# Attention of a two-layer hybrid block: one score product per head, exponentials turned by TensorE, values as the stationary operand

## The chip, the cores and the metric

The kernel runs on one core of a Trainium2 chip. The metric is the device time of one execution in microseconds (us). A core has TensorE (PE in the rows; its weight loads are PEld), VectorE (DVE), ScalarE (ACT), GpSimd (POOL) and SyncE (SP). TensorE takes both operands from SBUF and writes its products to PSUM, of which there are eight banks of 128 x 512 fp32 values. Two number formats matter here: `F32R`, with which a product is one TensorE instruction, and `F32`, with which a product shows as two instructions in the trace.

## The reference, cut to what matters

The model has two layers over 256 context tokens and 256 latent tokens of width 1024. A layer is a SwiGLU block, a mixer and a SwiGLU block. The mixer has three groups: attention (512 features, 8 query heads of 64, 2 key/value heads), a gated linear recurrence (LRU, 256 features) and a short convolution (256 features). In layer 0 both streams have queries; in layer 1 only the latent one has.

```python
def attend(q, k, v):
    s = jnp.einsum('bqkgd,bskd->bkgqs', q, k, preferred_element_type=jnp.float32) * ATTN_SCALE
    p = jax.nn.softmax(s, axis=-1).astype(v.dtype)
    return jnp.einsum('bkgqs,bskd->bqkgd', p, v)

def merge_groups(parts, g, w_out):
    return jnp.concatenate([_rms(t) for t in parts], axis=-1) * g @ w_out
...
    k_all = jnp.concatenate([kc, kx], axis=1)     # 256 context keys, then 256 latent keys
    attn_x = blocked_attention(qx, k_all, v_all)  # latent queries: 512 keys
...
    attn_c = attend(qc, kc, vc)                   # context queries: 256 keys, layer 0 only
```

## The kernel before

Activations lie with features on the partitions and tokens along the free dimension: columns 0 to 255 are the context (`CS`, s = 0), 256 to 511 the latent tokens (`XS`, s = 1). An fp32 product of weights and activations is made of three `F32R` products of high and low parts (`mm3`, L326 to L330), so nearly all TensorE work of the kernel stands in lines 328 to 330. Every weight block of 128 x 1024 is loaded by SP, then split by ACT (high part, L120) and DVE (low part, L121), two blocks ahead of its use.

A mixer is a list of steps in an order written out by hand (`ORDER`, L27 to L35); every engine's instructions follow that list, apart from small interchanges that the framework makes when it lays the engines' queues out ahead of time. The steps around the change are: `sc` the convolution's three projections per feature tile, `qc` the turning of queries, `ga` and `ge` the gates of the LRU, `lr` and `ls` its roots and scans, `me` the norms of LRU (1) and convolution (0), `op` the share of these two groups in the output projection (needs both `me`). `kT` holds the keys as [high; high] and [low; low], `qT` the queries as [high; low], both with head features on the partitions, so that two `F32R` products make a score.

The attention steps of one stream and head, before:

- `mx` (`maxima`, L788): scores with queries on the partitions and keys along the free dimension, for four heads; DVE takes the negative maximum over the keys (L802) and nothing else of them is kept.
- `mr` (`max_rows`, L806): the maxima are turned into rows by TensorE (L814) and copied by ACT (L817).
- `sm` (`softmax`, L820): the scores a second time, now with keys on the partitions (L828), plus a third product of 8 rows that adds the head's maximum (L830, `sel` and `mrows`); ACT takes the exponential (L832).
- `va` (`values`, L836): the exponentials are the stationary operand, `vp` (64 values and a column of ones) the moving one, 65 columns wide (L845), both in `F32`. The last head of four divides by the sum (L852, L853).
- `rn` (`row_norm`, L856) and `co` (`columns`, L870): the group's norm with tokens on the partitions, then four turns back to features on the partitions (L876), gains and the split into high and low parts.

After the steps come the attention group's products of the output projection (`out_attn`, L924), first for the context, then for the latent stream.

Of the kernel before, what the change touches and what calls it, by code (L numbers as in the profile page):

```python
# [25 lines left out]
# the order of a mixer's steps after its first products, by layer  # L26
ORDER = ((  # L27
# [8 lines left out]

# columns of the packed per-feature parameters
# [43 lines left out]
def plan():  # L81
    # the first two modules: features 512.. by products ("p"), the others as all modules
# [12 lines left out]
def hybrid_block_kernel(ctx: ExitStack, tc, wpk, xin, pp, cc, cct, qkg, rope, lruw, ident, out):  # L95
# [116 lines left out]
    def lru_consts():  # L212
        # -8 softplus(-lam), halved:  softplus(y) = max(y, 0) + log1p(exp(-|y|))
# [850 lines left out]
```

## Time and profile before

| what | value |
|---|---|
| time, median of 3 runs | 1772.7 us (1772.56 to 1773.01) |
| span of the profiled execution, first to last instruction | 1770.9 us |
| what lies around that span, against the median | 1.8 us |
| PE busy in the span | 1733.4 us (98%) |
| DVE, ACT busy in the span | 1111.8 us (63%), 644.0 us (36%) |
| attention of layer 0, first `mx` to the end of `co` | 484.06 to 624.06 us |
| attention of layer 1, first `mx` to the end of `op` | 1449.39 to 1550.30 us |

All rows come from one profiled execution, and times in them count from the start of its span. A matmul's busy time in the groups of instructions includes its latency, and matmuls overlap; how long one holds TensorE is read from the chain of waits, which gives each piece of time to one instruction. The granted clock of TensorE is given as a share: 1.00 is 2.4 GHz, 0.50 is 1.2 GHz, and a stretch with both shows a number between.

### The profile page before, as it was taken

Reading aid. Unit: us, or ns where it says so; the run is one execution under the profiler, and the core shown is the slowest. Engines: PE = TensorE matmul, PEld = TensorE weight load, DVE = VectorE, ACT = ScalarE, POOL = GpSimd, SP = SyncE. Lnnn points to the kernel's source line nnn. Section 1 sums busy time; section 2 is a strip of 40 time slices with the busy share of each in tenths; the row PEclk is TensorE's granted clock in tenths of the full one; section 3 lists DMA queues with packets and bytes.
Section 4 is the critical chain, followed back from the end, with each engine's and each line's share of the span. In section 5 each row is a group of like instructions: output and inputs, shape, how many; then the busy total and the mean of one; then the engine's idle time right before and its main releaser. Section 6 shows DMA issues by size and latency. Waiting matters only on the chain.

```text
span 1770.9 us, 22767 instructions
## 1 busy us (share of the span) xinstructions
PE 1733.4 (98%) x9098; PEld 1475.1 (83%) x9098; DVE 1111.8 (63%) x1872; ACT 644.0 (36%) x967; POOL 0.2 (0%) x4
## 2 busy tenths in 40 slices
PE   7999999999999999999999999999999989999997
PEld 2888888888877898888888898888888877889997
DVE  5977666776754276685667665754565685265555
ACT  5332122325832253322223343212232474254343
POOL 0000000000000000000000000000000000000000
PEclk9999999999987799999999999999999996699999
DMA  7465544552210024554454434443444221035551
GB/s 284 166 202 191 181 161 170 190 179 96 85 46 1 25 72 147 172 196 162 156 183 170 157 107 143 168 153 133 149 147 166 87 98 55 24 129 200 184 181 46
DMA packets 67938, 246.28 MB, mean 139 GB/s; under 512 B 7668, under 2 KB 8180, under 8 KB 67576
## 3 DMA queue, kind: packets, MB, share of 16 engines
q1 hardware_dynamic: 66816, 243.82, 40.1%
q8 instruction: 71, 1.16, 0.3%
q10 hardware_dynamic: 1016, 1.01, 0.2%
q14 instruction: 35, 0.29, 0.0%
HBM read 243.76 MB, written 1.05 MB: 138 GB/s over the span
## 4 chain that ended last, share of the span: by engine, by line
PE 92%; DVE 4%; ACT 2%; DMA 1%; issue 0%; ACTq 0%; DVEq 0%; SPq 0%
PE ps L328 27%; PE ps L329 27%; PE ps L330 27%; PE ps L845 3%; PE ps L828 2%; PE ps L830 2%; PE ps L799 1%; PE ps L376 1%; DVE junk L253 1%; DVE lo L121 1%; PE ps L749 1%; ACT hh L408 1%; DMA xT<-in_xin_dram 1%; DVE hl L409 1%; DVE ht L407 0%; ACT hi L120 0%
## 5 line engine op out<-in xcount | busy, mean ns | idle before, releaser
L120 ACT ACTIVATE hi<-raw 128x1024 fp32r<-128x1024 f32 x310 | 327.3, 1060 | 799.2 <-PE ps L329 589.0
L328 PE MATMUL ps<-hh,hi 128*128 128x512 f32 (+1 forms) x1664 | 574.9, 352 | 9.2 <-ACT hh L408 9.1
L329 PE MATMUL ps<-hl,hi 128*128 128x512 f32 (+1 forms) x1664 | 582.3, 351 | 1.1 <-DVE hl L409 0.9
L330 PE MATMUL ps<-hh,lo 128*128 128x512 f32 (+1 forms) x1664 | 579.5, 350 | 0.0
L121 DVE TENSOR_TENSOR lo<-raw,hi 128x1024 fp32r<-128x1024 f32 x310 | 378.1, 1222 | 202.3 <-ACT hi L120 201.5
L328 PEld LDWEIGHTS ps<-hh,hi 128*128 128x128 f32 x1664 | 313.0, 191 | 53.4 <-ACT hh L408 12.6
L329 PEld LDWEIGHTS ps<-hl,hi 128*128 128x128 f32 x1664 | 317.0, 191 | 44.1 <-DVE hl L409 3.3
L330 PEld LDWEIGHTS ps<-hh,lo 128*128 128x128 f32 x1664 | 317.2, 191 | 40.2
L253 DVE SCALAR_TENSOR_TENSOR junk<-raw,cb 128x1024 bf16<-128x1024 f32 x272 | 321.1, 1218 | 12.1 <-DMA raw<-in_wpk_dram 12.0
L328 PE MATMUL ps<-gh,hi 128*128 128x512 f32 (+1 forms) x770 | 267.4, 347 | 0.0
L329 PE MATMUL ps<-gl,hi 128*128 128x512 f32 (+1 forms) x770 | 266.9, 347 | 0.0
L330 PE MATMUL ps<-gh,lo 128*128 128x512 f32 (+1 forms) x770 | 266.8, 347 | 0.0
L487 DVE TENSOR_TENSOR gf<-gf,ps 128x512 f32<-128x512 f32 (+1 forms) x88 | 54.5, 619 | 180.1 <-PE ps L330 179.0
L329 PEld LDWEIGHTS ps<-gl,hi 128*128 128x128 f32 x770 | 145.8, 189 | 18.3
L328 PEld LDWEIGHTS ps<-gh,hi 128*128 128x128 f32 x770 | 145.8, 189 | 18.2
L330 PEld LDWEIGHTS ps<-gh,lo 128*128 128x128 f32 x770 | 145.8, 189 | 18.0
L417 DVE SCALAR_TENSOR_TENSOR xT<-ps,modT,xT 128x256 f32<-128x256 f32 x160 | 72.4, 479 | 91.4 <-PE ps L330 90.5
L408 ACT ACTIVATE hh<-ht,modT 128x256 fp32r<-128x256 f32 x88 | 41.9, 504 | 70.4 <-DVE ht L407 69.8
L845 PEld LDWEIGHTS ps<-vp,P 128*128 128x128 f32 x320 | 61.8, 295 | 2.4 <-issue 1.4
L845 PE MATMUL ps<-vp,P 128*128 128x65 f32 x320 | 62.6, 379 | 0.0
L357 ACT ACTIVATE sq<-xT 128x256 f32<-128x256 f32 (+1 forms) x62 | 29.0, 486 | 73.5 <-DVE xT L417 73.2
L121 DVE TENSOR_TENSOR gl<-gf,gh 128x512 fp32r<-128x512 f32 (+1 forms) x88 | 54.4, 618 | 0.7 <-ACT gh L120 0.7
(192 smaller groups left out, 1336.5 us busy)
## 6 DMA issues: line engine op xcount, KB each, us to landing
raw<-in_wpk_dram SPq DMA_DIRECT2D x456, 512.0 KB, 3.3
xT<-in_xin_dram SPq DMA_DIRECT2D x2, 1024.0 KB, 9.6
lw<-in_lruw_dram SPq DMA_DIRECT2D x2, 512.0 KB
cb<-in_cc_dram SPq DMA_DIRECT2D x2, 512.0 KB, 3.6
out_dram<-y SPq DMA_DIRECT2D x2, 256.0 KB, 2.6
out_dram<-y ACTq DMA_DIRECT2D x2, 256.0 KB, 2.6
pps<-in_pp_dram ACTq DMA_DIRECT2D x1, 138.0 KB, 4.6
qkb<-in_qkg_dram ACTq DMA_DIRECT2D x1, 128.0 KB
```

The source lines that it names most:

```text
L120: act(hi, src, AF.Copy)
L121: tt(lo, src, f(hi), OP.subtract)
L253: stt(junk, raw, 1.0, CB[v], op0=OP.mult, op1=OP.mult, accum_out=mod_col(l, m, t, v))
L328: nc.tensor.matmul(ps, wh, xh, start=first, stop=False)
L329: nc.tensor.matmul(ps, wh, xl, start=False, stop=False)
L330: nc.tensor.matmul(ps, wl, xh, start=False, stop=last)
L408: act(hh[:, a:b], t[:, a:b], AF.Identity, bias=mod_col(l, 3 * n, k, v))
L417: stt(xT[:, k, a:b], ps[:, a:b], mod_col(l, m, k, v), xT[:, k, a:b], op0=OP.mult, op1=OP.add)
L487: tt(gf[:, a:b], gf[:, a:b], pu[:, a:b], OP.mult)
L828: nc.tensor.matmul(o, kT[2 * g + z][:, kc:kc + 128], qT[s, hd], start=z == 0, stop=False)
L830: nc.tensor.matmul(o, sel[:, hd % 4, :], mrows[s, g], start=False, stop=True)
L845: nc.tensor.matmul(pv[s][t][:, j * 65:(j + 1) * 65], p[:, t * 128:(t + 1) * 128], vp[:, kt, g], start=kt == 0, stop=kt == len(P) - 1)
```

## The change

Scores are computed once per head (`scores`), with queries on the partitions, as `maxima` did. DVE takes the negative maximum of the bank, and ACT takes the exponential out of the same bank with that maximum as its bias, and sums each row as it goes (`accum_out`). `max_rows`, the second score products, the 8-row products and `sel` are gone. For a pair of heads (`turned`) TensorE turns the exponentials, 128 x 128 at a time, so that keys lie on the partitions, four into a bank; ACT and DVE copy the banks to SBUF by turns. The values are now the stationary operand: `vz` holds the 64 values of a key tile between two blocks of 64 zeros, and a window of 128 columns over it puts a head's output on the lower or the upper 64 partitions. The moving operand is the turned exponentials of two heads, 512 columns wide, in `F32`; two pairs of a key/value head add up in one bank (`values`). The output thus has features on the partitions at once. The inverse row sums are spread over 64 features each, turned (`inverses`) and multiplied in (`merge_attn`), which then takes the group's norm with products of ones, like the other groups, and splits. The order of the steps is written anew from the first score step on.

```diff
 ORDER = ((
...
-    "cv0 cv1 kv0 kv1 ga0 ga1 ga3 ga2 qp0 qp1 kr ge0 ge1 qp2 qp3 qr0 lr sc0 sc1 kc ls0 sc2 qc0 qr1 mx0 sc3 "
-    "sc4 sc5 mr0 sm0 sm2 mx1 va0 qc1 mr1 sm1 sm4 va2 sm3 ls1 sm7 va1 me1 sm6 sm5 va3 va4 mx2 me0 mr2 sm8 "
-    "va5 sm10 sm9 mx3 op0 mr3 va6 sm11 sm12 va8 op1 va9 va7 sm15 op2 va10 op3 op4 sm14 sm13 rn0 va11 va12 "
-    "va14 va13 co0 va15 rn1 op5 op6 op7 co1"),
+    "cv0 cv1 kv0 kv1 ga0 ga1 ga3 ga2 qp0 qp1 kr ge0 ge1 qp2 qp3 qr0 lr sc0 sc1 kc ls0 sc2 qc0 qr1 sm0 sc3 "
+    "sm2 sm1 tr0 sc4 sm3 sm4 va0 sc5 tr1 sm6 qc1 sm5 va1 tr2 ls1 sm7 sm8 va2 tr3 me1 sm10 sm9 va3 nr0 tr4 "
+    "sm11 rn0 sm12 va4 tr5 me0 sm14 sm13 va5 tr6 op0 sm15 va6 tr7 nr1 op1 op2 va7 op3 rn1 op4 op5 op6 op7"),
     (
-    "cv0 kv0 kv1 kr qp0 qp1 qp2 qp3 qr1 ga0 qc1 sc0 cv1 sc1 ge0 sc2 kc ga1 mx0 sc3 ga3 ga2 sc4 sc5 mr0 "
-    "mx1 ge1 sm3 sm0 sm1 sm2 lr mr1 ls0 va0 va1 me0 ls1 sm6 sm5 sm4 va2 va3 sm7 va4 va6 me1 va5 op0 va7 "
-    "op1 rn0 op2 op3 co0 op4 op5 op6 op7"))
+    "cv0 kv0 kv1 kr qp0 qp1 qp2 qp3 qr1 ga0 qc1 sc0 cv1 sc1 ge0 sc2 kc ga1 sm0 sc3 ga3 ga2 sm2 sc4 sm1 tr0 sc5 "
+    "sm3 ge1 sm4 va0 tr1 lr sm6 sm5 va1 tr2 ls0 sm7 me0 va2 tr3 ls1 nr0 me1 op0 va3 op1 rn0 op2 op3 op4 op5 op6 op7"))
...
-    vp = const.tile([128, 4, NKV, 65], F32, name="vp")
-    vec.memset(vp[:, :, :, 64:65], 1.0)
...
+    vz = const.tile([128, 4, NKV, 192], F32, name="vz")
+    nc.gpsimd.memset(vz, 0.0)
...
             nc.tensor.matmul(st[:, a:b], ones[n], x[:, a:b], start=i == 0, stop=i == len(parts) - 1)
+        return rstd_tail(st, cols)
+
+    def rstd_tail(st, cols):
+        a, b = cols
         r0, r1 = T(name="r0"), T(name="r1")
...
-                    act(vp[:, t, :, 0:64], pk[t][:, 128:256].rearrange("p (s d) -> p s d", s=2), AF.Copy)
+                    act(vz[:, t, :, 64:128], pk[t][:, 128:256].rearrange("p (s d) -> p s d", s=2), AF.Copy)
...
-        def maxima(s, hd):
...
-        def max_rows(s, hd):
...
-        def softmax(s, hd):
...
-        def values(s, hd, P):
...
-        def row_norm(s):
...
-        def columns(s):
...
+        def heads(p):
+            g, z = p // 2, p % 2
+            return g, z, (4 * g + z, 4 * g + 2 + z)
...
+        def scores(s, hd):
+            g = hd // 4
...
+            nb = const.tile([128, 2], F32, tag="nb", name="nb", bufs=6)
+            w = 256 if s == 0 else 512
+            n = 512 // w
+            P[s, hd] = []
+            for i in range(0, 2, n):
+                ps = bank()
+                for j in range(n):
+                    q = qT[s, hd][:, (i + j) * 128:(i + j) * 128 + 128]
+                    for z in range(2):
+                        nc.tensor.matmul(ps[:, j * w:(j + 1) * w], q, kT[2 * g + z][:, 0:w], start=z == 0, stop=z == 1)
+                vec.tensor_reduce(nb[:, i:i + n], ps.rearrange("p (i c) -> p i c", i=n), axis=AX.X, op=OP.max, negate=True)
+                p = T(name="P")
+                for j in range(n):
+                    act(p[:, j * w:(j + 1) * w], ps[:, j * w:(j + 1) * w], AF.Exp, bias=nb[:, i + j:i + j + 1],
+                        accum_out=sums[s][:, i + j, hd:hd + 1])
+                    P[s, hd].append(p[:, j * w:(j + 1) * w])
+
+        def turned(s, p):
+            hds = heads(p)[2]
+            PT[s, p] = []
+            for k in range(2 if s == 0 else 4):
+                ps = bank()
+                for j, hd in enumerate(hds):
+                    for i in range(2):
+                        c = j * 256 + i * 128
+                        nc.tensor.transpose(ps[:, c:c + 128], P[s, hd][i][:, k * 128:(k + 1) * 128], idf)
+                t = T(name="PT")
+                if flip[0] % 2:
+                    vec.tensor_copy(t, ps)
+                else:
+                    act(t, ps, AF.Copy)
+                flip[0] += 1
+                PT[s, p].append(t)
+
+        def values(s, p):
+            g, z, _ = heads(p)
+            if z == 0:
+                pv[s, g] = bank()
+            pts = PT.pop((s, p))
+            for k, t in enumerate(pts):
+                nc.tensor.matmul(pv[s, g], vz[:, k, g, 64 - 64 * z:192 - 64 * z], t,
+                                 start=z == 0 and k == 0, stop=z == 1 and k == len(pts) - 1)
+
+        def inverses(s):
+            r = const.tile([128, 2, NH, 1], F32, tag="ri", name="ri", bufs=2)
+            vec.reciprocal(r[:, :, :, 0], sums[s])
...
+            for i, x in enumerate((e, e2)):
+                act(x.rearrange("p (h d) -> p h d", h=NH), r[:, i].to_broadcast([128, NH, 64]), AF.Copy)
+            rec[s] = []
+            for g in range(2):
+                ps = bank()
...
+                        nc.tensor.transpose(ps[:, c:c + 128], x[:, k * 128:(k + 1) * 128], idf)
+                t = T(name="rec")
+                act(t, ps, AF.Copy)
+                rec[s].append(t)
+
+        def merge_attn(s):
+            a, b = parts[s]
+            ot, sq = [], []
+            for g in range(2):
+                o, x = T(name="ot"), T(name="sq")
+                tt(o, pv.pop((s, g)), rec[s][g], OP.mult)
+                act(x, o, AF.Square)
...
+            st = bank()
+            for i, x in enumerate(sq):
+                nc.tensor.matmul(st[:, 0:256], ones[512], x, start=i == 0, stop=i == 3)
...
+                rs = rstd_tail(st, (0, 256))
+            for k, o in enumerate(ot):
+                stt(o, o, grn[:, l, k:k + 1], rs[:, 0:256], op0=OP.mult, op1=OP.mult)
+                split(mg[k][0][:, a:b], mg[k][1][:, a:b], o)
...
-            "mx": lambda i: maxima(*items[4 * i]), "mr": lambda i: max_rows(*items[4 * i]),
-            "sm": start, "va": lambda i: values(*items[i], P.pop(i)), "lr": lambda i: lru_roots(), "ls": lru_scan,
-            "rn": lambda i: row_norm(items[8 * i][0]), "co": lambda i: columns(items[8 * i][0]),
+            "sm": lambda i: scores(*items[i]), "tr": lambda i: turned(*pairs[i]), "va": lambda i: values(*pairs[i]),
+            "nr": lambda i: inverses(pairs[4 * i][0]), "rn": lambda i: merge_attn(pairs[4 * i][0]),
+            "lr": lambda i: lru_roots(), "ls": lru_scan,
```

## Rows read from the trace of the kernel before

**Rows 1.** Profile page: TensorE's granted clock in 40 slices, the chain's shares by engine
```profile
PEclk9999999999987799999999999999999996699999
...
PE 92%; DVE 4%; ACT 2%; DMA 1%; issue 0%; ACTq 0%; DVEq 0%; SPq 0%
```

**Rows 2.** Attention stretches: us; busy PE, PEld, DVE, ACT, POOL (count); clock; DMA share; GB/s
```profile
484.06:624.06 140.00, 137.56 (x618) 109.42 (x619) 61.75 (x135) 44.82 (x85) 0.00 (x0) 0.82 0.09 31
1449.39:1550.30 100.91, 100.86 (x456) 83.37 (x455) 47.71 (x95) 44.12 (x80) 0.00 (x0) 0.68 0.13 42
```

**Rows 3.** Chain of waits, shares by line: 484.06 to 624.06 us, then 1449.39 to 1550.30
```profile
by line: PE ps L845 23.3%; PE ps L828 15.4%; PE ps L830 11.9%; PE ps L328 10.2%; PE ps L329 9.7%; PE ps L330 9.7%; PE ps L799 9.3%; PE ps L376 3.8%; PE ps L876 1.8%; DVE nb L802 1.8%; PE ps L683 1.0%; DVE uc L890 0.9%; DVE ml L121 0.4%; DVE
by line: PE ps L845 25.7%; PE ps L828 20.3%; PE ps L830 14.8%; PE ps L328 7.7%; PE ps L799 7.3%; PE ps L329 6.9%; PE ps L330 6.9%; PE ps L749 4.3%; PE ps L376 3.6%; PE ps L876 0.9%; ACT mh L120 0.4%; PE ps L814 0.4%; DVE uc L890 0.4%; DVE o
```

**Rows 4.** Chain pieces (start us, us, what): softmax products, then value products, two clocks
```profile
510.83 0.43 PE ps L828 x2
511.27 0.31 PE ps L830
...
583.92 1.73 PE ps L845 x16
...
1520.83 7.02 PE ps L845 x32
```

**Rows 5.** Chain pieces: F32R 512 and 256 wide, F32 turns, F32 512 wide
```profile
1422.26 0.23 PE ps L330
...
432.02 0.12 PE ps L329
...
623.18 0.88 PE ps L876 x8
...
436.22 6.87 PE ps L749 x16
```

**Rows 6.** Groups of instructions: busy us, mean ns of one, idle before them
```profile
L832 ACT ACTIVATE P<-ps 128x512 f32<-128x512 f32 x40 | 23.4, 596 | 48.5 <-PE ps L830 48.5
L802 DVE TENSOR_REDUCE nb<-ps 128x1 f32<-128x512 f32 x32 | 20.5, 682 | 9.6 <-PE ps L799 9.6
...
L859 ACT ACTIVATION_READ_ACCUMULATOR sq<-orow 128x1 f32 x6 | 1.1, 188 | 0.0
```

**Rows 7.** Busy time by stretch: early and late part of each attention
```profile
484.00:512.00 28.00, 27.94 (x159) 23.53 (x159) 24.63 (x52) 12.95 (x26) 0.00 (x0) 1.00 0.28 95
512.00:624.00 112.00, 109.56 (x460) 85.83 (x460) 37.12 (x83) 31.87 (x61) 0.00 (x0) 0.77 0.04 15
1449.40:1470.00 20.60, 20.60 (x120) 16.88 (x118) 18.76 (x33) 18.60 (x29) 0.00 (x0) 1.00 0.39 128
1470.00:1550.00 80.00, 79.94 (x336) 66.18 (x336) 28.93 (x63) 25.39 (x51) 0.00 (x0) 0.59 0.06 20
```

**Rows 8.** Order of time, layer 1: the LRU's table load on ACT, its last DVE step
```profile
1467.64 1.28 ACT L572 ACT_TABLE_LOAD   x1
...
1498.71 0.42 DVE L782 SCALAR_TENSOR_TENSOR uc<-uc,ge 128x256 f32<-128x256 f32 x1
```

**Rows 9.** Busy time and clock: F32 gates of layer 0, attention of layer 1
```profile
436.20:443.10 6.90, 6.90 (x18) 3.07 (x17) 2.56 (x3) 6.80 (x12) 0.00 (x0) 1.00 0.79 287
...
1474.30:1539.10 64.80, 64.75 (x226) 52.47 (x226) 15.83 (x36) 16.49 (x37) 0.00 (x0) 0.50 0.03 9
```

**Rows 10.** Chain pieces: turns and value products around the clock's rise
```profile
611.02 0.85 PE ps L876 x4
...
612.19 0.85 PE ps L876 x4
613.05 1.86 PE ps L845 x12
```

**Rows 11.** Order of time, PE in layer 1: an idle gap; chain piece after it
```profile
1434.08 0.81 PE L683 MATMUL ps<-idr,qr 128*128 128x128 f32 x4 [5.12 <-DVE qr L121]
...
1436.29 0.21 PE ps L328
```

More of the change, by code (lines that the diff above doesn't have):

```diff
@@ L785, in mixer @@
         mg = [(T(F32R, "mh"), T(F32R, "ml")) for _ in range(KD)]
-        nbs, mrows, pv, orow = {}, {}, {}, {}
-        def maxima(s, hd):
-            g = hd // 4
-            nb = const.tile([128, 2, 4], F32, tag="nb", name="nb", bufs=3)
-            for j in range(4):
-                hd = 4 * g + j
-                for t in ([(0, 1)] if s == 0 else [(2,), (3,)]):
-                    w = 512 // len(t)
-                    ps = bank()
-                    for i, q in enumerate(t):
-                        for z in range(2):
-                            nc.tensor.matmul(ps[:, i * w:(i + 1) * w], qT[s, hd][:, q % 2 * 128:q % 2 * 128 + 128],
-                                             kT[2 * g + z][:, 0:w], start=z == 0, stop=z == 1)
-                    o = t[0] % 2
-                    vec.tensor_reduce(nb[:, o:o + len(t), j], ps.rearrange("p (i c) -> p i c", i=len(t)),
-                                      axis=AX.X, op=OP.max, negate=True)
-            nbs[s, g] = nb
@@ L806, in max_rows @@
-        def max_rows(s, hd):
-            g = hd // 4
-            nb = nbs.pop((s, g))
-            nz = const.tile([128, 2, 2, 4], F32R, tag="nz", name="nz", bufs=3)
-            vec.tensor_copy(nz[:, :, 0], nb)
-            tt(nz[:, :, 1], nb, f(nz[:, :, 0]), OP.subtract)
-            ps = bank()
-            for i in range(2):
-                nc.tensor.transpose(ps[0:8, i * 128:(i + 1) * 128].bitcast(F32R),
-                                    nz[:, i].rearrange("p z h -> p (z h)"), idr)
-            mr = const.tile([8, 256], F32R, tag="mr", name="mr", bufs=3)
-            act(mr, ps[0:8, 0:256], AF.Copy)
-            mrows[s, g] = mr
@@ L820, in softmax @@
-        def softmax(s, hd):
-            g, P = hd // 4, []
-            for k0 in range(0, 2 if s == 0 else 4, 2):
+        P, PT, pv, rec, sums = {}, {}, {}, {}, {}
+        flip = [0]
+        def heads(p):
+            g, z = p // 2, p % 2
+            return g, z, (4 * g + z, 4 * g + 2 + z)
+        def scores(s, hd):
+            g = hd // 4
+            if s not in sums:
+                sums[s] = const.tile([128, 2, NH], F32, tag="sums", name="sums", bufs=2)
+            nb = const.tile([128, 2], F32, tag="nb", name="nb", bufs=6)
[14 more added lines that the diff above has]
+                    P[s, hd].append(p[:, j * w:(j + 1) * w])
@@ L824, in softmax @@
                 ps = bank()
                 for j in range(2):
-                    kc, o = (k0 + j) * 128, ps[:, j * 256:(j + 1) * 256]
-                    for z in range(2):
-                        nc.tensor.matmul(o, kT[2 * g + z][:, kc:kc + 128], qT[s, hd],
-                                         start=z == 0, stop=False)
-                    nc.tensor.matmul(o, sel[:, hd % 4, :], mrows[s, g], start=False, stop=True)
-                p = T(name="P")
-                act(p, ps, AF.Exp)
@@ L833, in softmax @@
-                P += [p[:, 0:256], p[:, 256:512]]
-            return P
-        def values(s, hd, P):
-            g, j = hd // 4, hd % 4
-            if j == 0:
-                pv[s] = [bank(), bank()]
-            if hd == 0:
-                orow[s] = [T(name="orow") for _ in range(2)]
-            for t in range(2):
-                for kt, p in enumerate(P):
-                    nc.tensor.matmul(pv[s][t][:, j * 65:(j + 1) * 65], p[:, t * 128:(t + 1) * 128], vp[:, kt, g],
-                                     start=kt == 0, stop=kt == len(P) - 1)
-            if j < 3:
-                return
-            for t in range(2):
-                v = pv[s][t][:, 0:260].rearrange("p (h d) -> p h d", d=65)
-                r = const.tile([128, 4, 1], F32, tag="ri", name="ri", bufs=4)
-                vec.reciprocal(r, v[:, :, 64:65])
-                tt(orow[s][t][:, g * 256:(g + 1) * 256].rearrange("p (h d) -> p h d", d=64), v[:, :, 0:64],
-                   r.to_broadcast([128, 4, 64]), OP.mult)
@@ L856, in row_norm @@
-        def row_norm(s):
-            v, x, y = (const.tile([128, 2], F32, tag=f"on{i}", name="on") for i in range(3))
-            for t in range(2):
-                act(T(name="sq"), orow[s][t], AF.Square, accum_out=v[:, t:t + 1])
-            ts(v, v, 1.0 / 512, EPS, op0=OP.mult, op1=OP.add)
-            ln(x, v)
-            act(x, x, AF.Exp, scale=-0.5)
-            tt(y, x, x, OP.mult)
-            tt(y, y, v, OP.mult)
-            ts(y, y, -0.5, 1.5, op0=OP.mult, op1=OP.add)
-            tt(y, y, x, OP.mult)
-            for t in range(2):
-                act(orow[s][t], orow[s][t], AF.Copy, scale=y[:, t:t + 1])
@@ L870, in columns @@
-        def columns(s):
-            a, b = parts[s]
-            for k in range(4):
-                ps = bank()
-                for t in range(2):
-                    nc.tensor.transpose(ps[:, t * 128:(t + 1) * 128], orow[s][t][:, k * 128:(k + 1) * 128], idf)
-                g = par(P_GRP + l * 8 + k)
-                act(mg[k][0][:, a:b], ps[:, 0:256], AF.Copy, scale=g)
-                stt(mg[k][1][:, a:b], ps[:, 0:256], g, f(mg[k][0][:, a:b]), op0=OP.mult, op1=OP.subtract)
+                    for i, x in enumerate((e, e2)):
+                        c, k = j * 256 + i * 128, 2 * g + j
+                        nc.tensor.transpose(ps[:, c:c + 128], x[:, k * 128:(k + 1) * 128], idf)
@@ L902, in out_part @@
             residual(l, 5, m, ps, oc)
-        P = {}
         items = [(s, hd) for s in range(1 if last else 0, 2) for hd in range(NH)]
-        def start(i):
-            P[i] = softmax(*items[i])
+        pairs = [(s, p) for s in range(1 if last else 0, 2) for p in range(4)]
         steps = {
```

10 lines of the change are left out of this document (6 added, 4 removed).

## The prediction

> **What bounds the kernel now.** I read the chain of waits by engine first: 92% of the span is TensorE, and the granted clock by slice falls in two places only, both of them the attention of a layer [rows 1]. So a change to attention is worth what it does to TensorE's queue there. Busy time by stretch says how long the two stretches are: 140.0 us in layer 0 (first `mx` to the last `co`) and 100.9 us in layer 1 (first `mx` to the last `op`), with TensorE busy all through, DVE for 61.8 and 47.7 us, ACT for 44.8 and 44.1 us, at mean clocks of 0.82 and 0.68 [rows 2]. The chain's shares by line say what fills them [rows 3]. In layer 0 the value products (L845) hold 23.3% or 32.6 us, the second score products (L828) 15.4% or 21.6, the 8-row products (L830) 11.9% or 16.7, and the turns back (L876) 1.8% or 2.5. In layer 1 the same four are 25.9, 20.5, 14.9 and 0.9 us. Together that is 135.6 of 240.9 us, and all of it goes with the change.
>
> The reader should see why these lines are so dear. A softmax tile of two 256-wide products and the 8-row one takes 0.43 + 0.31 = 0.74 us at full clock [rows 4], where three 256-wide `F32R` products in a plain stream take 3 x 0.12 us [rows 5]. A value record moves 65 columns, and 16 of them take 1.73 us at full clock and 32 take 7.02 at half (0.108 and 0.219 each) [rows 4]. Layer 1 ran 64.8 us of this at a clock of 0.50 without a break [rows 9].
>
> **The change part by part, on TensorE.** I price the new queue at full clock from rows of the same form, and count the instructions from the diff. The forms [rows 5]: `F32R` 512 wide 0.23 us, 256 wide 0.12; a 128 x 128 `F32` turn 0.88 / 8 = 0.11; an `F32` record 512 wide 6.87 / 16 = 0.43, two records to a product, so 0.86; an `F32` product 256 wide is taken as half of that, 0.43.
>
> Layer 0, new or rewritten: scores 32 x 0.12 + 32 x 0.23 = 11.2; turns of exponentials 32 + 64 = 96 x 0.11 = 10.6; value products 8 + 16 = 24 x 0.86 = 20.6; inverse sums turned 16 x 0.11 = 1.8; sums of squares 8 x 0.43 = 3.4. That is 47.6 us. Kept in the same stretch: `sc` 72 x 0.23 = 16.6, `qc` 16 x 0.11 (the dearer kind of turn) = 1.8, `me` 4 x 0.86 = 3.4, `op` 96 x 0.23 = 22.1, together 43.9. Sum 91.5 against 140.0: 48.5 less.
>
> Layer 1, latent stream only and 256 wide: scores 32 x 0.23 = 7.4, turns 64 x 0.11 = 7.0, values 16 x 0.86 = 13.7, inverses 0.9, squares 4 x 0.43 = 1.7, together 30.7. Kept: `sc` 72 x 0.12 = 8.6, gates 4 x 0.86 = 3.4, `me` 4 x 0.43 = 1.7, `op` 96 x 0.12 = 11.5, together 25.2. Sum 55.9 against 100.9: 45.0 less.
>
> So a TensorE that neither waits nor slows gives 93.5 us. The value products alone hardly shrink (34.3 us now, 58.5 before, most of those at half clock); the rest comes from the second scores and the 8-row products, 73.7 us, which are paid back with 17.6 us of turns.
>
> **The clock.** The old streams ran at half clock for most of layer 1, and the sum takes the new one at full. For the value products the nearest row is the gates of layer 0: 16 records of just this form, 6.9 us with nothing between them, at 1.00 [rows 9]. For the turns it is the end of layer 0's attention: four turns in 0.85 us and four again (half clock), then twelve value records in 1.86 us, 0.155 each, which lies between the two levels [rows 10, 4]. So the clock rose to full where TensorE had run turns and value products only. A turn there does not hold the clock down. The Trainium skill says the opposite: "TensorE: Matmul & The Clock Gate", Part 4 (PE-mode transpose), has it that transposes don't count as activity for the clock gate and that the full clock doesn't engage for them. By that rule this change, with 160 more turns, would run much of attention at half clock; by the row it would not. It is the first rival below.
>
> **The change beside TensorE.** ACT in layer 1 gains 16 sum reads at 0.19, 8 copies of turned banks at 0.60 and 6 further 512-wide passes (spreading, copying, squares) at 0.60 [rows 6]: 3.0 + 4.8 + 3.6 = 11.4, and loses `row_norm`'s four passes, 2.4; the narrow ones about cancel. 44.1 + 9 = 53 us. DVE gains 8 copies and 2 multiplications at 0.68 [rows 6] and three narrow passes at half of it, 7.8, and loses some 2 of small ones: 47.7 + 6 = 54 us. Both have to fit beside 55.9 us of TensorE work, where they had 100.9. In layer 0 the same count gives DVE +9.5 to 71 and ACT +16 to 61 us beside 91.5. So TensorE stays the longest, but in layer 1 by a hair only, and waits must be added.
>
> Layer 0: in the first 28 us DVE was busy for 24.6 [rows 7], with the rotation of the latent queries and the scans. The new order brings TensorE from `sm0` to `sm7` in 28 us and adds three bank copies, 2 us, to that DVE work. I take 3 us of waits there and 3 in the rest, 6 in all; bounds 0 (the order covers all, as it does now) and 12 (each of eight pairs waits for a reduction and a sum read more).
>
> Layer 1: DVE and ACT were busy for 18.8 and 18.6 of the first 20.6 us [rows 7], and the LRU's chain runs through them. Its table load on ACT came at 1467.64 and its last DVE step at 1498.71 [rows 8]. In the new order five score steps and two `tr` stand ahead of `lr`, on ACT 10 x (0.60 + 0.19) + 4 x 0.60 = 10.3 us: the load goes to about 1478. Eight root passes, two more score steps and two copies on ACT (9 us), scans of which some 7 us come last, and the norm's chain of about 4 us (four ACT and five DVE passes, narrow) put the first `op` near 1498; all `op` and the sums of squares then take 13.2 us, to about 1511 or 1512. That is 62.5 us, not 55.9: 7 us of waits ahead of `op0`. Behind them stand all `op` steps and the attention group's products. An idle gap can cost the clock as well: after 5.12 us without work, 256-wide products ran at 0.21 us [rows 11]. I add 4 us for that. 11 us in layer 1; bounds 0 and 20.
>
> **Edits at nothing.** The bank of a score is now held for product, reduction and exponential, some 2 us; eight banks (two for values, two or three under turns, the rest for scores) cover that while TensorE spends 3.4 us on a pair's values. If they don't, it is in the bounds above. The zeroing of `vz` is on POOL, long ahead of its first use by ACT. Loads, their order and SP's queue don't change; DMA is at 0.09 and 0.13 in the stretches [rows 2], so earlier requests find it free. The dropped constants (`sel`, the ones of `vp`) are less than 1 us beside other work.
>
> **The sum.** Span 1770.9 - 93.5 + 6 + 11 = 1694.4, and with 1.8 us around the span 1696 us, 4.3% less than the median of 1772.7. Waits between 0 and 32 us give 1679 to 1711.
>
> **Rivals.**
> (1) TensorE at half clock in attention, by the page's rule. The new attention steps are 47.6 + 30.7 = 78.3 us at full clock; at half a turn takes 0.21 instead of 0.11 [rows 10] and a 256-wide product 0.21 instead of 0.12 [rows 11, 5], so they would grow by about 0.9, 70 us, and hide the waits: 1679 + 70 = 1749. If only half of them run so: 1679 + 35 + some waits, near 1722. For it: the clock was low in both stretches [rows 9]. Against it: rows 9 and 10, as told. Chance 0.20, from 1711 to 1751.
> (2) The order hides every wait, DVE and ACT being below TensorE in each sum: 1679. Against it: how close they are in layer 1. Chance 0.09.
> (3) Slower: the pair's chain lies bare. From a pair's last score to its values stand a reduction (0.68), an exponential with its sum (0.78) and a bank copy (0.60 to 0.68) [rows 6]; if each of 12 pairs waits for all of it, that is 26 us, and with rival 1 in full 1749 + 26 = 1775. It decides only if the half clock comes together with over 24 us of such waits. Against it: the order puts at least one other score step, and mostly a `va`, between. Chance 0.04.
>
> **How the numbers follow.** The forecast (full clock, 10 to 32 us of waits, 1684 to 1711) has 0.66, rival 1 0.20, rival 2 0.09 (1676 to 1684), rival 3 0.04, and 0.01 stays for less than that. The range from 1678 to 1732 takes in the forecast, most of rival 2 and the lower half of rival 1, and leaves out about 0.16. A measurement of this kernel tells 0.2% (3.5 us) from no change: faster 0.94, same 0.02, slower 0.04.
>
> **What would show it.** Right: value records 512 wide at 0.43 and turns at 0.11 us in the chain, the clock near 1.0 in layer 0's attention, stretches of about 97 and 67 us, DVE or ACT as what ends TensorE's idle time before `tr` and before `op0` of layer 1. Wrong: turns at 0.21 (rival 1), no idle time (rival 2), idle time before every `tr` (rival 3). Most of all, the forecast fails if turns in a denser stream than those of the row lower the clock.

## The result, and the profile of the changed kernel

The changed kernel takes 1730.6 us in the median of four runs (1729.5 to 1732.1), beside 1772.9 us for the kernel before on the same chip: a ratio of 0.977, with a 95% interval of 0.975 to 0.979. That is 42 us less; the forecast was 76 us less. Of all the runs told here one was slow, at a lower granted clock: a run of e7 of 1744.2 us, which e7's median leaves out. The profiled execution is the run of 1732.1 us, and its page begins so (span; PE busy, share, count; granted clock by slice):

```profile
span 1730.3 us, 22217 instructions
...
PE 1659.9 (96%) x8790; PEld 1405.6 (81%) x8790; DVE 1128.7 (65%) x1869; ACT 661.4 (38%) x1036; POOL 1.6 (0%) x5
...
PEclk9999999999988999999999999999999999999999
```

The two dips of [rows 1] are nearly gone, but PE's share of the span fell from 98 to 96%: about 70 us of the span have no matmul in them, where there were 37.5. The two attention stretches, layer 0's from 3 us ahead of its first `sm0`, layer 1's from its first `sm0`, both to the last `op` product (columns as in [rows 2]):

```profile
484.00:612.50 128.50, 104.59 (x458) 77.08 (x457) 75.22 (x139) 59.73 (x140) 0.00 (x0) 0.89 0.11 37
1437.06:1509.50 72.44, 62.61 (x332) 48.38 (x331) 54.01 (x97) 50.22 (x102) 0.00 (x0) 0.93 0.16 52
```

The first `sm0` of layer 0 is at 487.18 us, and the output products of attention begin at 612.35: 125.2 us against a forecast of 97. Layer 1 takes 72.4 against 67. In both, PE now stands idle: 24 us and 10 us. What PE waited for, in layer 0 from 487 us on and in layer 1 from 1437 us on (line that waited, who released it: us in total, times, longest):

```profile
PE ps L823 <- ACT P L810: 11.8, 2, 8.4
PE ps L856 <- ACT re L849: 7.4, 1, 7.4
PE ps L872 <- ACT sq L867: 2.5, 1, 2.5
PE ps L839 <- ACT PT L828: 2.0, 3, 1.2
...
PE ps L370 <- ACT acc L348: 3.7, 1, 3.7
PE ps L322 <- ACT mh L118: 3.4, 1, 3.4
PE ps L823 <- ACT P L810: 2.8, 2, 2.5
```

(L823 turns the exponentials, L856 the inverse sums, L872 sums squares, L839 multiplies values, L370 sums squares of the two other groups.) All of it waits for ACT, and most of layer 0's idle time lies in three waits: 8.4, 7.4 and 3.4 us.

**The wait of 8.4 us, before `tr0`.** In order of time, first PE, then DVE, then ACT (start us, us, engine, line, operation, out<-in, count, idle time before and who ended it):

```profile
502.73 1.15 PE L823 MATMUL ps<-idf,P 128*128 128x128 f32 x4 [8.39 <-ACT P L810]
...
488.84 0.67 DVE L807 TENSOR_REDUCE nb<-ps 128x2 f32<-128x512 f32 x1
...
495.25 0.68 DVE L807 TENSOR_REDUCE nb<-ps 128x2 f32<-128x512 f32 x1
...
500.79 0.68 DVE L618 TENSOR_TENSOR qo<-qo,hr 128x512 f32<-128x512 f32 x1
...
496.56 0.72 ACT L118 ACTIVATE qr<-qo 128x256 fp32r<-128x256 f32 x2 [2.30 <-DVE qo L618]
501.50 0.72 ACT L118 ACTIVATE qr<-qo 128x256 fp32r<-128x256 f32 x2 [4.22 <-DVE qo L618]
502.13 0.45 ACT L810 ACTIVATE P<-ps,nb 128x256 f32<-128x256 f32 x1
```

The maxima of `sm0` are ready at 489.5 us, and its first exponential runs at 502.13. ACT isn't busy meanwhile: it idles 2.30 and 4.22 us at the splits of `qr1` (high parts of the rotated latent queries, L118), which wait for DVE's rotation (L618), and 2.49 us before that at the roots of the same step (L572). DVE is busy for all of these 12.6 us. The exponentials stand behind those splits in ACT's queue. The Trainium skill says as much in "PSUM — Partial Sum Buffer", Engine vs sequencer instructions: the queues of ScalarE, VectorE and GpSimd are strictly first in, first out. The rows agree: 12.6 us passed with the input ready.

**The wait of 7.4 us, before `nr0`.** The same view, DVE first, then ACT, then PE:

```profile
538.68 1.41 DVE L889 SCALAR_TENSOR_TENSOR uc<-uc,grn,r 128x512 f32<-128x512 f32 x2
...
539.47 1.29 ACT L118 ACTIVATE mh<-uc 128x512 fp32r<-128x512 f32 x2 [4.21 <-DVE uc L889]
540.67 0.67 ACT L810 ACTIVATE P<-ps,nb 128x512 f32<-128x512 f32 x1
...
543.32 1.15 ACT L849 ACTIVATE re<-ri 128x512 f32<-128x512 f32 x2
...
544.01 2.06 PE L856 MATMUL ps<-idf,re 128*128 128x128 f32 x8 [7.43 <-ACT re L849]
```

Here it is the split of `me1` (the LRU group's norm, L118 called by `merge`) that waits 4.21 us for DVE's scaled result (L889). Four exponentials and the spreading of the inverse sums stand behind it. The wait of 3.4 us stands behind the split of `me0` in the same way.

**The clock.** Three stretches from `qr1`'s wait to `me1`'s, with the columns of [rows 2]:

```profile
498.10:508.30 10.20, 5.57 (x17) 4.22 (x18) 5.88 (x13) 4.43 (x16) 0.00 (x0) 0.50 0.16 53
508.30:539.00 30.70, 27.43 (x132) 19.43 (x131) 16.07 (x27) 14.78 (x38) 0.00 (x0) 1.00 0.11 35
539.00:549.30 10.30, 5.29 (x25) 5.07 (x26) 3.14 (x5) 7.36 (x16) 0.00 (x0) 0.50 0.00 0
```

TensorE has the full level (2.4 GHz) for 30.7 us and the half level (1.2 GHz) in a stretch that begins in each of the two long gaps. There are two more such stretches in layer 0 (552.7 to 556.1 and 576.6 to 580.0) and three in layer 1 (10.2 us together), each behind a shorter gap. In layer 0 that is 27 us at half clock with PE busy for 17.5 of them, so about 9 us lost; in layer 1 about 5.

### The profile page after: what moved, and what is told of

The parts are those of the page before. It is cut to its first block, busy times and chain, and to the rows that moved or that the text cites. A ratio compares the mean times of both kernels' runs of the same rounds, so it can differ in the third digit from the quotient of the medians.

```text
span 1730.3 us, 22217 instructions
## 1 busy us (share of the span) xinstructions
PE 1659.9 (96%) x8790; PEld 1405.6 (81%) x8790; DVE 1128.7 (65%) x1869; ACT 661.4 (38%) x1036; POOL 1.6 (0%) x5
## 5 line engine op out<-in xcount | busy, mean ns | idle before, releaser
L118 ACT ACTIVATE hi<-raw 128x1024 fp32r<-128x1024 f32 x310 | 327.2, 1060 | 796.5 <-PE ps L323 586.8
L322 PE MATMUL ps<-hh,hi 128*128 128x512 f32 (+1 forms) x1664 | 576.4, 353 | 9.3 <-ACT hh L406 9.1
L324 PE MATMUL ps<-hh,lo 128*128 128x512 f32 (+1 forms) x1664 | 581.5, 351 | 0.0
L322 PEld LDWEIGHTS ps<-hh,hi 128*128 128x128 f32 x1664 | 314.0, 191 | 53.6 <-ACT hh L406 12.6
L324 PEld LDWEIGHTS ps<-hh,lo 128*128 128x128 f32 x1664 | 318.4, 191 | 40.5
L247 DVE SCALAR_TENSOR_TENSOR junk<-raw,cb 128x1024 bf16<-128x1024 f32 x272 | 321.2, 1220 | 12.6 <-DMA raw<-in_wpk_dram 12.6
L322 PE MATMUL ps<-gh,hi 128*128 128x512 f32 (+1 forms) x770 | 267.4, 347 | 0.0
L324 PE MATMUL ps<-gh,lo 128*128 128x512 f32 (+1 forms) x770 | 266.9, 347 | 0.0
L322 PEld LDWEIGHTS ps<-gh,hi 128*128 128x128 f32 x770 | 145.8, 189 | 18.2
L324 PEld LDWEIGHTS ps<-gh,lo 128*128 128x128 f32 x770 | 145.8, 189 | 18.0
L415 DVE SCALAR_TENSOR_TENSOR xT<-ps,modT,xT 128x256 f32<-128x256 f32 x160 | 72.4, 479 | 69.6 <-PE ps L324 68.5
L407 DVE SCALAR_TENSOR_TENSOR hl<-ht,modT,hh 128x256 fp32r<-128x256 f32 x88 | 40.6, 482 | 20.9 <-ACT hh L406 20.8
L322 PE MATMUL ps<-mh,hi 128*128 128x256 f32 (+1 forms) x160 | 50.9, 319 | 3.4 <-ACT mh L118 3.4
```

The costliest lines, as they stand in the source:

```text
L118: act(hi, src, AF.Copy)
L247: stt(junk, raw, 1.0, CB[v], op0=OP.mult, op1=OP.mult, accum_out=mod_col(l, m, t, v))
L322: nc.tensor.matmul(ps, wh, xh, start=first, stop=False)
L324: nc.tensor.matmul(ps, wl, xh, start=False, stop=last)
L407: MADE.append(stt(hl[:, a:b], t[:, a:b], mod_col(l, 3 * n, k, v), f(hh[:, a:b]), op0=OP.add, op1=OP.subtract).ins)
L415: stt(xT[:, k, a:b], ps[:, a:b], mod_col(l, m, k, v), xT[:, k, a:b], op0=OP.mult, op1=OP.add)
```

## The experiments

Three theories were put to the chip. A: single splits at the head of ACT's in-order queue, which wait for DVE, hold up the exponentials behind them; the gaps this makes on PE then cost clock too. B: ACT (in e1 and e6 also DVE) simply has too much work for the shorter stretch. C: the turns on TensorE hold the clock down (rival 1). Each set of runs has the kernel before beside it on its own chip, so ratios are compared; the medians of before were 1777.7 us (e1, e2, e3, e5), 1774.4 (e4, e6, e7, e8) and 1771.0 (e0, e9, e10).

Lengths below are taken between the starts of the same two weight products in every trace: the 2101st and the 2305th of L322 to L324 for layer 0, the 6201st and the 6501st for layer 1. Between the two layers lie 789 us and from the end of the second to the last of these products 207.3 to 208.5, in every kernel, so nearly all differences are in these two lengths and in the start. The lengths are of one trace each; two traces of the changed kernel differ by 0.6 us in layer 0.

| kernel | median us | ratio to before (95%) | layer 0 us | layer 1 us |
|---|---|---|---|---|
| before | 1772.9 | | 146.4 | 135.2 |
| the change | 1730.6 | 0.977 (0.975 to 0.979) | 131.7 | 105.8 |
| the change again (e0) | 1732.2 | 0.978 (0.976 to 0.981) | 131.1 | 105.8 |
| e1 `qr1` later | 1719.7 | 0.968 (0.964 to 0.972) | 119.3 | 104.7 |
| e2 `me1` later | 1732.0 | 0.975 (0.972 to 0.978) | 131.3 | 105.7 |
| e3 turns x 4 | 1769.5 | 0.996 (0.994 to 0.997) | 154.1 | 121.1 |
| e4 no sums | 1728.7 | 0.975 (0.972 to 0.977) | 131.5 | 104.9 |
| e5 filler | 1725.4 | 0.971 (0.968 to 0.974) | 124.7 | 105.8 |
| e6 merge on DVE | 1720.2 | 0.970 (0.967 to 0.972) | 122.7 | 106.2 |
| e7 e1 and e6 | 1708.8 | 0.964 (0.961 to 0.966) | 109.3 | 104.7 |
| e8 e7, new order in layer 1 | 1706.6 | 0.962 (0.959 to 0.965) | 109.0 | 103.9 |
| e9 e7, gaps filled | 1707.5 | 0.965 (0.962 to 0.968) | 112.7 | 103.0 |
| e10 e7, copies on DVE | 1710.2 | 0.966 (0.964 to 0.968) | 109.2 | 106.5 |

### e1: `qr1` behind `tr0`

```
-    "... ls0 sc2 qc0 qr1 sm0 sc3 "
-    "sm2 sm1 tr0 sc4 sm3 ..."
+    "... ls0 sc2 qc0 sm0 sc3 "
+    "sm2 sm1 tr0 qr1 sc4 sm3 ..."
```

> Against the changed kernel's 1730.6 us. Theory A (the exponentials stand on ACT's in-order queue behind the splits of the latent queries, which wait for DVE): with the step qr1 put behind tr0, TensorE's wait of 8.4 us before the first turns of layer 0 falls below 2 us, and the stretch at half clock that follows it goes; 8 to 11 us less, 1720 to 1723. Theory B (DVE has too much to do there, whatever the order): the wait turns up again at qc1 or tr1; less than 2 us gained.

Layer 0 is 12.4 us shorter. ACT's first exponential in order of time, then the stretch up to 511.6 us (columns as in [rows 2]):

```profile
491.35 0.47 ACT L810 ACTIVATE P<-ps,nb 128x256 f32<-128x256 f32 x1 [0.96 <-DVE nb L807]
```

```profile
484.00:511.60 27.60, 27.51 (x144) 22.46 (x143) 25.46 (x46) 15.10 (x36) 0.00 (x0) 1.00 0.31 107
```

The exponential now waits for its own maxima and nothing else, PE is busy for 27.5 of 27.6 us, and the clock is 1.00. DVE is as full as the forecast feared (25.5 of 27.6 us), but TensorE no longer waits for it. The gain is more than the 8.4 us of the wait: most of the rest is the clock that the gap had cost. The edit moves the whole step, with DVE's rotation: in the changed kernel `sm2`'s maxima, which `tr0` needs too, were ready at 495.9 us, 1.6 us after PE ran out of work. So up to some 2 us of the 8.4 (an estimate) may be due to DVE's order and not to ACT's, which e1 doesn't separate.

### e2: `me1` behind `sm11`

```
-    "... va2 tr3 me1 sm10 sm9 va3 nr0 tr4 "
-    "sm11 rn0 ..."
+    "... va2 tr3 sm10 sm9 va3 nr0 tr4 "
+    "sm11 me1 rn0 ..."
```

> Against the changed kernel's 1730.6 us. Theory A (ACT's queue stands behind the split of the LRU's norm, which waits for DVE, with four exponentials and the spreading of the inverse sums behind it): with me1 put behind nr0, tr4 and sm11, the wait of 7.4 us before the turns of the inverse sums falls below 2 us; 5 to 9 us less, 1722 to 1726. Theory B (ACT itself is too full): the wait turns up again before rn0 or tr5; less than 2 us gained.

No gain. PE's waits in layer 0:

```profile
PE ps L823 <- ACT P L810: 11.8, 2, 8.4
PE ps L872 <- ACT sq L867: 7.7, 1, 7.7
...
PE ps L856 <- ACT re L849: 1.2, 1, 1.2
```

The wait before `nr0` fell from 7.4 to 1.2 us, as A has it, but the one before the squares' sums of `rn0` grew from 2.5 to 7.7: `rn0`'s squares now stand behind the same split (and wait 1.36 us more for DVE's products). A step that waits in an in-order queue has to go where nothing urgent follows it; here every place has something urgent behind it. Expected was a gain, and the expectation was wrong: what came is what it had for B (the wait turns up again before `rn0`, less than 2 us gained). By itself this run doesn't speak for A; e6, which takes the split off ACT, does.

### e3: every turn of exponentials four times

```
-                        nc.tensor.transpose(ps[:, c:c + 128], P[s, hd][i][:, k * 128:(k + 1) * 128], idf)
+                        for _ in range(4):
+                            nc.tensor.transpose(ps[:, c:c + 128], P[s, hd][i][:, k * 128:(k + 1) * 128], idf)
```

> Every turn of exponentials is done four times, 480 turns more, in bursts of 64 in layer 1. Theory A (turns keep the clock, only idle gaps lose it): 480 x 0.11 = 53 us more, less 10 to 20 us of waits that it hides: 1763 to 1774; turns at 0.11 us, clock 1.00 inside the bursts. Theory C (turns don't count for the clock): turns at 0.21 us, all 640 of them: 480 x 0.21 + 160 x 0.10 = 117 us more, some 1835 to 1850, clock 0.50 in the bursts.

480 more turns cost 37.7 us in the two layers (22.4 + 15.3), less than the 52.3 us that 480 x 0.109 makes, since some 9 us of them lie in what were waits (38.6 us in the two lengths before, 29.6 now) and the clock is at half for less of PE's work (23.4 us against 31.6), which is worth 4. A chain piece of layer 1 (L824 is the turn), then its stretch (columns as in [rows 2]):

```profile
1485.78 6.99 PE ps L824 x64
```

```profile
1485.78:1492.70 6.92, 6.92 (x65) 6.92 (x64) 4.34 (x7) 6.25 (x11) 0.00 (x0) 1.00 0.23 76
```

64 turns in a row take 6.99 us, 0.109 each, and the clock through them is 1.00. So C falls: turns hold the full clock. By the page's rule (the Trainium skill, "TensorE: Matmul & The Clock Gate", Part 4) a burst of nothing but turns would be the place for the half clock; the measurement decides against it here.

### e4: no sums of the exponentials

```
-                        accum_out=sums[s][:, i + j, hd:hd + 1])
...
+                nc.gpsimd.memset(sums[s], 256.0)
```

> Leaves out the row sums that ACT takes with each exponential (the sums are a constant 256 instead), 48 reads of 0.19 us less on ACT. Theory B (ACT is too full in the attention): up to 9 us less, 1722 from the changed kernel's 1730.6. Theory A (ACT loses its time in instructions that wait for DVE, with the exponentials behind them): the waits before tr0 and nr0 stay within 1 us of 8.4 and 7.4; at most 3 us less, 1728 to 1731.

48 sum reads leave ACT. A read overlaps the exponential before it (by 0.09 us in the first of layer 0), so that this takes only 2.6 us of ACT's busy time from layer 0 (60.8 to 58.2), less than half of the 32 x 0.19 that was expected. PE's first two waits in layer 0:

```profile
PE ps L823 <- ACT P L811: 11.6, 2, 8.3
PE ps L856 <- ACT re L849: 7.1, 1, 7.1
```

They hardly move, and layer 0 is 131.5 us against 131.1 to 131.7. Taking this work from ACT brings nothing that can be told from the 0.6 us between two traces: against B in layer 0, though the dose is small. e7 below weighs more.

### e5: unread products in the two gaps

```
+        def filler(n):
+            ps = bank()
+            for _ in range(n):
+                nc.tensor.matmul(ps, ones[512], vz[:, 0:2].rearrange("p k g c -> p (k g c)")[:, 0:512], start=True, stop=True)
...
+    "sm2 sm1 fi8 tr0 ... va3 fi8 nr0 tr4 "
```

> Adds 16 products of F32, 512 wide (13.8 us at full clock), whose result nobody reads: eight before tr0 and eight before nr0 of layer 0, where TensorE waits 8.4 and 7.4 us. Theory A (idle gaps lose the clock, and that costs what runs behind them): the added work lies in the waits and the clock stays at 1.00 behind them; 3 to 6 us less than 1730.6 although there is more work. Theory C (the turns and the new products themselves lose the clock): half clock there as before, and the time is the same or up to 14 us more.

16 more `F32` products, 13.8 us of TensorE work whose result nobody reads, make layer 0 7.0 us shorter (6.4 against e0's trace). The two stretches around the gaps and the waits that are left of them (L828 is the turn here, L861 the inverses'):

```profile
484.20:509.20 25.00, 23.43 (x108) 16.71 (x107) 22.37 (x43) 13.40 (x33) 0.00 (x0) 1.00 0.30 104
538.00:560.00 22.00, 17.81 (x79) 11.17 (x78) 13.73 (x26) 14.47 (x35) 0.00 (x0) 1.00 0.00 0
```

```profile
PE ps L828 <- ACT P L810: 4.9, 2, 3.4
PE ps L861 <- ACT re L854: 0.6, 1, 0.6
```

ACT and DVE do the same work as before, and the exponentials come no earlier. What changed is that TensorE didn't stand still, and the clock stayed at 1.00 where it was 0.50. So the half clock of the changed kernel is a consequence of the gaps, and costs several us of its own.

### e6: the high part of `me0` and `me1` on DVE

```
-                split(mg[k][0][:, a0:], mg[k][1][:, a0:], p[:, a0:])
+                vec.tensor_copy(mg[k][0][:, a0:], p[:, a0:])
+                tt(mg[k][1][:, a0:], p[:, a0:], f(mg[k][0][:, a0:]), OP.subtract)
```

> The high parts of the LRU's and the convolution's norm are written by DVE (eight more passes there) instead of by ACT, so that ACT has no instruction in me0 and me1 that waits for DVE's share of the norm. Theory A (that wait on ACT's in-order queue is what holds up the exponentials, and the wait before nr0 only moved to rn0 when me1 was put later, because me1 still stood ahead of something): the waits before nr0 (7.4 us) and the second half of tr6 (3.4 us) fall by half or more; 5 to 10 us less than 1730.6. Theory B (DVE or ACT has too much to do): DVE has more work, so no gain, or up to 4 us more.

DVE writes the high part itself, right behind the scaled result, so ACT has no instruction that waits for it. PE's waits in layer 0:

```profile
PE ps L823 <- ACT P L810: 8.4, 1, 8.4
PE ps L856 <- ACT re L849: 2.9, 1, 2.9
PE ps L872 <- ACT sq L867: 2.3, 1, 2.3
```

7.4 became 2.9, the 3.4 us before `tr6` are gone, and the 8.4 of `qr1`, which wasn't touched, stays. Layer 0 is 9.0 us shorter, with more work on DVE. Layer 1 gains nothing.

### e7: e1 and e6 together

> qr1 behind tr0 and the high parts of both norms on DVE. Theory A: the two gains add, 12 to 20 us less than 1730.6, 1711 to 1719; TensorE's waits in layer 0 under 8 us in all. Theory B: no more than the first of them gave, about 1718 to 1721.

The two gains add: layer 0 is 22.4 us shorter (12.4 + 9.0 alone), and the median 21.8 us below the changed kernel's, a little more than the 12 to 20 that were expected. What is left of its waits, and then the length of layer 0 as in the table, first in the changed kernel, then in e7 (columns as in [rows 2]):

```profile
PE ps L856 <- ACT re L849: 2.9, 1, 2.9
PE ps L872 <- ACT sq L867: 2.4, 1, 2.4
...
```

```profile
484.25:615.95 131.70, 107.79 (x486) 80.34 (x485) 77.94 (x143) 60.79 (x141) 0.00 (x0) 0.90 0.11 37
484.59:593.86 109.27, 101.85 (x485) 75.60 (x484) 79.73 (x147) 58.41 (x136) 0.00 (x0) 0.98 0.14 44
```

ACT and DVE together are busy for 138.7 and 138.1 us (the high parts of two norms changed hands), yet the layer is 22 us shorter. What differs is what stands at the head of ACT's queue. So neither engine's load made the 22 us: against B.

### e8, e9: other orders on top of e7

e8 takes the LRU's and the short convolution's steps of layer 1 earlier:

```
-    "... ga3 ga2 sm2 sc4 sm1 tr0 sc5 "
-    "sm3 ge1 sm4 va0 tr1 lr sm6 sm5 va1 tr2 ls0 sm7 me0 va2 tr3 ls1 nr0 me1 op0 va3 ..."
+    "... ga3 ga2 ge1 sm2 sc4 sm1 lr tr0 sc5 "
+    "sm3 ls0 sm4 va0 tr1 sm6 ls1 sm5 va1 tr2 me0 sm7 va2 me1 tr3 nr0 op0 va3 ..."
```

> As e7_both, and in layer 1 the last gate, the LRU's roots and scans and me0, me1 come earlier in the order, ahead of most score steps. Theory A: the waits of 3.7 us before me0's sums and 3.4 us before op0 go, and the half clock behind them; 5 to 10 us less than e7_both. Theory B (ACT's early part of layer 1 is full, 20 of 20 us): the exponentials come later by as much, and the waits move to tr0 and tr1; within 3 us of e7_both.

Layer 1 is 0.8 us shorter. Its two waits of 3.7 and 3.6 us (e7) are gone, and in their place stand, among others:

```profile
PE ps L839 <- ACT PT L828: 3.4, 1, 3.4
...
PE ps L839 <- DVE PT L826: 2.6, 1, 2.6
```

e9 puts `op0` to `op4` of layer 0 between its last attention steps, `me0` earlier in both layers:

```
-    "... sm7 sm8 va2 tr3 me1 sm10 sm9 va3 nr0 tr4 "
-    "sm11 rn0 sm12 va4 tr5 me0 sm14 sm13 va5 tr6 op0 sm15 va6 tr7 nr1 op1 op2 va7 op3 rn1 op4 op5 op6 op7"),
+    "... sm7 me0 sm8 va2 tr3 me1 sm10 sm9 va3 op0 nr0 op1 tr4 "
+    "sm11 op2 rn0 sm12 va4 tr5 sm14 sm13 op3 va5 tr6 op4 sm15 va6 tr7 nr1 op5 op6 va7 op7 rn1"),
...
-    "... tr2 ls0 sm7 me0 va2 tr3 ls1 ..."
+    "... tr2 me0 ls0 sm7 va2 tr3 ls1 ..."
```

> As e7_both (1709 us, ratio 0.9636), and the order of layer 0 has me0 and me1 earlier and op0 to op4 set between the score, turn and value steps; in layer 1 me0 stands ahead of sm7. Theory A (what is left in layer 0 is TensorE having nothing to do while ACT and DVE are not full): the waits of 2.9, 2.4 and 1.5 us in layer 0 and 3.7 us in layer 1 shrink to under 3 us in all, and the half clock behind them goes: 6 to 12 us less than e7_both. Theory B (ACT and DVE are full): within 3 us of e7_both.

The waits before `nr0` and `rn0` shrink to 0.6 us, and new ones come (L890 is the high part that `op0` multiplies):

```profile
PE ps L322 <- DVE mh L890: 4.8, 1, 4.8
PE ps L370 <- ACT acc L348: 2.5, 1, 2.5
```

Theory A's 5 to 10 us (e8) and 6 to 12 us (e9) didn't come. e8's median is some 2 us below e7's on the same chip; e9 makes layer 0 3.4 us longer and layer 1 1.7 us shorter. Once the two large waits are gone, moving steps by hand in these two ways mostly moved the remaining ones.

### e10: every turned bank of layer 1 copied by DVE

```
-                if flip[0] % 2:
+                if l == 1 or flip[0] % 2:
```

> As e7_both, and in layer 1 all 16 turned banks are copied by DVE: 8 x 0.60 us less on ACT, 8 x 0.69 us more on DVE. Theory B for layer 1 (ACT is full from 1412 to 1445 us, and everything later in that layer is late by it): layer 1 gets 2 to 5 us shorter. Theory A (waits by order): layer 1 stays within 1.5 us, or grows by up to 4 us as the copies queue behind DVE's scans.

If ACT's load set layer 1, it should shrink. The same 80 us of layer 1, first e7, then e10 (busy PE, PEld, DVE, ACT):

```profile
1405.00:1485.00 80.00, 70.01 (x404) 55.50 (x403) 59.51 (x106) 58.60 (x115) 0.00 (x0) 0.95 0.17 53
```

```profile
1405.00:1485.00 80.00, 69.69 (x390) 54.34 (x389) 62.46 (x113) 53.20 (x106) 0.00 (x0) 0.93 0.17 53
```

ACT lost 5.4 us of work, and layer 1 came 1.8 us longer, with 4.3 us of wait at `me0`'s sums instead of 3.7. So ACT's load alone doesn't set layer 1 either. The work went to DVE, so e10 doesn't tell whether the two engines together do. What remains there (8 to 10 us of gaps and 3 to 5 of clock, behind the first `sm0`) is left open: neither an earlier order (e8, e9) nor less work on ACT (e10) took it away.

### e0: the changed kernel again

> The changed kernel itself, beside the others of this set. Ratio to the kernel before near 0.977 again; of its start (up to the first product of the first norm, 31.3 us before and 33.2 after in the profiled runs) between 31 and 36 us, since that place differs between kernels that are alike there.

Its waits are the same (11.8, 7.4, 2.5 and 2.0 us). Its first weight product starts at 32.0 us, against 33.2 in the first trace. Over all kernels of this study, whose code up to there is the same, that moment lies between 31.3 us (the kernel before) and 35.6 us, so differences of a few us between two single traces say nothing on their own.

## Why the prediction was right, and where it fell short

The direction and the range were right, and the time fell between the forecast of 1696 us and the range's upper end of 1732. That the range held is in part luck: the forecast itself ended at 1711, and what lay above it stood for the lower half of rival 1, whose mechanism didn't come. The time got there by waits in layer 0 of twice their upper bound. The gap to the profiled 1732.1 us is 36 us: 27.8 in layer 0 (14.7 gained, 42.5 forecast), 4.6 in layer 1 (29.4 gained, 34 forecast), and 3 in the time up to layer 0's attention, 2 of which are in the start.

**TensorE's sum: right.** Prices in the changed kernel, as chain pieces of layer 1 (start us, us, what):

```profile
1460.28 3.44 PE ps L839 x8
1463.71 1.76 PE ps L823 x16
...
1499.14 1.73 PE ps L872 x8
```

Eight value records in 3.44 us are 0.43 each, sixteen turns in 1.76 are 0.11, eight 256-wide records of squares in 1.73 are 0.216, where half of 0.43 was taken. These are the figures of [rows 5]. Less the waits and what the clock cost, layer 0 is 125.2 - 23.7 - 9 = 92.5 us (91.5 in the sum) and layer 1 72.4 - 9.9 - 5 = 57.5 (55.9). With the two large waits removed (e7), layer 0 is 37.1 us shorter than before, 5.4 us from the forecast's 42.5, with some 7 us of waits (the forecast had 6).

**The clock: right in cause, incomplete.** Turns and value products keep the full clock, as read from [rows 9, 10], and e3 shows it for bursts of turns alone. As evidence [rows 10] was thin: its eight turns all ran at half clock, and the clock rose behind them. That an idle gap can cost the clock was read from [rows 11] and priced at 4 us in layer 1 (it was about 5), but at nothing in layer 0, where it was about 9. A gap is not the only way to lose the clock: the old steps ran 64.8 us at 0.50 with TensorE busy throughout [rows 9], and no run here shows which of them did that. By the mean clocks of [rows 2] (0.82 and 0.68) the old attention lost some 25 and 32 us to the half clock, the new one 9 and 5. So, as an estimate, the change brought some 43 us of clock and 31 us of shorter work in the two stretches and gave 31 us back in waits; together these make the 43 us by which the stretches became shorter.

**DVE's and ACT's sums: right.** Forecast 71 and 61 us in layer 0, 54 and 53 in layer 1; measured, from the first `sm0` on, 72 and 57, 54 and 50. The step that failed came after them.

**The waits in layer 0: the failed step.** "I take 3 us of waits there and 3 in the rest, 6 in all; bounds 0 [...] and 12 (each of eight pairs waits for a reduction and a sum read more)". They were 23.7 us, and with the clock that they cost 33: the term is 27 us too small, which is nearly the whole shortfall of layer 0 (27.8). The bound was built from a wait that repeats with each pair. What came were three single waits, of 8.4, 7.4 and 3.4 us, at places that have nothing to do with pairs. The prediction compared ACT's busy time with the length of the stretch, and asked whether DVE was too full around the rotation of the latent queries. It didn't ask what stands ahead of the exponentials in ACT's queue and what that waits for. The rows of before couldn't show the cost, since TensorE didn't depend on ACT there at the same points; the order in the diff could: `qr1` stands right ahead of `sm0`, and `me1` ahead of `sm10` and `nr0`. That this is the cause, and not ACT's load or the turns, is shown by e1 and e6 (12.4 us back by moving the step with the first split, up to some 2 of which may be DVE's order, and 9.0 by taking the other two off ACT) against e7 (as much work on ACT and DVE together, and 22 us shorter), e4 (a little less work on ACT, nothing back) and e3 (turns keep the clock).

**Layer 1: right within 5 us.** Forecast were 7 us of waits ahead of `op0` and 4 of clock; measured 9.9 and 5. The place was only half right. The forecast followed the LRU's chain to `op0`, 48.6 us behind the first `sm0`; `op0` came 57.2 us behind it. In order of time, the LRU's last result on DVE, its squares on ACT, `op0` on PE:

```profile
1479.37 0.42 DVE L780 SCALAR_TENSOR_TENSOR uc<-uc,ge 128x256 f32<-128x256 f32 x1
...
1489.02 0.42 ACT L348 ACTIVATE acc<-uc 128x256 f32<-128x256 f32 x1
...
1494.28 0.50 PE L322 MATMUL ps<-mh,hi 128*128 128x256 f32 x2 [3.36 <-ACT mh L118]
```

The LRU is done 42.7 us behind `sm0`, about where the forecast had it (44.6, that is 4 us of norm ahead of 48.6). Its squares run 9.2 us later, as in ACT's queue the split of `me0`, two bank copies and the spreading and copying of the inverse sums stand ahead of them: the same pattern as in layer 0. What it costs in the end isn't settled, since e8, which puts `me1` ahead of `tr3`, gained no more than 0.8 us.

**The rivals.** Rival 1's range (1711 to 1751) holds the measured time, but its mechanism isn't there: of 160 turns in the changed kernel 134 run at the full clock, and those at half stand behind gaps. Rival 2 (no waits) and rival 3 (a wait at each pair) didn't come; the pairs' own chain costs 2.0 us in layer 0 (L839 for the turned bank).

The best kernels found are e7, e8 and e9, all within 3 us of each other, at ratios of 0.962 to 0.965: e7 needs one step moved and the high parts of two norms given to DVE.

## What to carry to other kernels

When a change puts an engine's work between two steps of the engine that sets the end, list what stands ahead of that work in its in-order queue and what each of those instructions waits for; a sum of busy times shows none of it. A conversion that waits for another engine's result can be done by the engine that made the result (e6; it paid in layer 0 and brought nothing in layer 1), or placed behind the urgent work (e1), and it has to be looked up what is urgent behind the new place (e2). An idle gap of TensorE can cost twice, once as time and once as clock (e5).

## What the runs showed of the hardware

- 64 turns of 128 x 128 `F32` blocks in a row run at 0.109 us each, at a granted clock of 1.00 (e3).
- 13.8 us of added, unread products made layer 0 some 7 us shorter, as TensorE kept its clock through two gaps (e5).
- ACT idled 4.2 us with ready work behind the instruction at its queue's head; 12.6 us passed from the maxima to the first exponential, in which ACT was busy for 2.9 us (changed kernel, `qr1`).
